# A batched matrix product in groups of four: order and run length of its loads, and which engine casts what

## The chip, the cores and the metric

The kernel runs on one core of a Trainium2 chip. Its engines each follow their own program: TensorE multiplies (PE in the profile, PEld for loading its stationary operand), VectorE (DVE), ScalarE (ACT) and GpSimd (POOL) do elementwise work, and SyncE (SP) here only issues transfers, which sixteen DMA engines carry out between the chip's main memory (HBM) and the core's memory (SBUF). Products arrive in PSUM. The engines meet at semaphores. The metric is device time in microseconds.

## What is computed

```python
# x: (8, 16, 256, 512) float32, weight: (8, 16, 512, 384) float32
def reference(x, weight):
    return np.matmul(x, weight).astype(np.float32)
```

That is 128 independent products of a 256x512 by a 512x384 matrix. The kernel reads 67.1 MB of x and 100.7 MB of weights, writes 50.3 MB, and multiplies in bf16.

## The kernel before

The 128 products are worked in NG = 32 groups of G = 4. Each SBUF tile has 128 partitions. A group's x is one transfer of 2 MB: partition p holds R = 8 consecutive rows of 512, so 32 partitions belong to each matrix (C = 32). A group's weights come in two transfers of 1.5 MB, two matrices each: partition p holds eight consecutive rows of 384, 12 KB, and 64 partitions belong to a matrix. A group's result is 1.5 MB, 12 KB per partition.

**Loads and stores (SyncE).** `on_sync` writes the order of the queue by hand. It first loads groups 0 to 3 (LAG = 4), then alternates load(n + 4) and store(n). `load` (L97 to L114) issues x (L101) and then the two halves of the weights (L109). There are two slots for x (XS = 2), four half slots for weights (WS = 4, so two groups) and four for results (OS = 4). Each issue waits until its slot is free: x until ScalarE has cast the x that lay there, weights until VectorE has cast theirs, a store (L122) until the group's result is copied. After the last load come stores 27 to 31; that of group 31 goes out in four pieces.

**VectorE** runs `prepare` for each group: eight casts of weights from fp32 to bf16 (L149, 64 partitions and 1536 elements each, the rows of a matrix being spread over all 128 partitions of w_bf), then four copies of transposed x from PSUM to x_t (L155), one for each pair of rows (T = 4). The casts wait for the weights' transfers, and for the multiplications of the group two before, which frees w_bf.

**TensorE** runs `multiply`: 16 transposes of x_bf (L168; pairs of bf16 numbers go through as one fp32 word), then 128 multiplications in four quarters (L182), with 32 columns of the array for each matrix. Quarter q waits for x_t's pair q and for the PSUM tile po (two of them), the first one also for all of the group's weight casts.

**ScalarE** copies each quarter from po to out_sb (`copy_out`, L196), and between quarters 1 and 2 casts the next group's x (`cast_x`, L131, two instructions of 2048 elements). There is one x_bf (BS = 1), so a cast of x waits for the transposes of the group before.

```python
        for n in range(rounds * U, NG):
            if n + LAG < NG:
                load(e, 0, NG, n + LAG)
            store(e, 0, NG, n, T if n == NG - 1 else 1)
```

Of the kernel before, what the change touches and what calls it, by code (L numbers as in the profile page):

```python
# [12 lines left out]
def kernel(  # L13
# [6 lines left out]
    nc = tc.nc  # L20
    P = 128

    b1, b2, M, K = x.shape
    _, _, _, N = weight.shape
    B = b1 * b2
    KO = K // P

    x_rows = x.rearrange("b1 b2 m k -> (b1 b2 m) k")
    w_rows = weight.rearrange("b1 b2 k n -> (b1 b2 k) n")
# [3 lines left out]
    bf16 = mybir.dt.bfloat16  # L33
# [6 lines left out]
    G = 4  # L40
    C = P // G
    R = G * M // P
    T = R // 2
    D = 2
    S = 2
    HP = P // D
    NG = B // G

    XS, WS, OS = 2, 2 * G // D, 4
    BS, TS, WBS = 1, 2, 2 * G  # L50
    PT, PO = 4, 2

    LAG = 4

    ctx.enter_context(tc.tile_critical(no_gpsimd_drain=True))  # L55

    def sbuf(name, shape, dtype, n):
        return [
            ctx.enter_context(nc.sbuf_tensor(f"{name}{s}", shape, dtype)) for s in range(n)
        ]  # L60
# [6 lines left out]
    def sems(name, n):  # L67
        return [tc.alloc_semaphore(f"{name}{s}") for s in range(n)]
# [2 lines left out]
    identity = sbuf("identity", [P, P], fp32, 1)[0]  # L71
    x_sb = sbuf("x_sb", [P, R, K], fp32, XS)

    x_bf = sbuf("x_bf", [P, R, S, HP, KO], bf16, BS)
    x_t = sbuf("x_t", [P, R, KO // 2, P, 2], bf16, TS)
    w_sb = sbuf("w_sb", [P, S * KO, N], fp32, WS)
    w_bf = sbuf("w_bf", [P, KO, N], bf16, WBS)
# [4 lines left out]

    id_done, x_cast, w_cast, t_made, t_copied, p_made, o_copied = (
        sems(name, 1)[0]
        for name in (
            "id_done", "x_cast", "w_cast", "t_made", "t_copied", "p_made", "o_copied"
        )
    )  # L90
    x_in, w_in, o_out = sems("x_in", XS), sems("w_in", WS), sems("o_out", OS)


    BIAS = 8


    def load(e, t, U, s):  # L97
        n = t * U + s
        if not isinstance(n, int) or n >= XS:
            e.wait_ge(x_cast, n + (1 - XS))  # L100
        e.dma_start(  # L101
            x_sb[s % XS][:],
            x_rows[bass.ds(n * (G * M), G * M)].rearrange("(p r) k -> p r k", r=R),
        ).then_inc(x_in[s % XS], 16)
        for d in range(G // D):
            slot = (s * (G // D) + d) % WS
            if not isinstance(n, int) or n >= 2:
                e.wait_ge(w_cast, n * (G * S) + ((d + 1) * D * S - 2 * G * S))  # L108
            e.dma_start(  # L109
                w_sb[slot][:],  # L110
                w_rows[bass.ds(n * (G * K) + d * (D * K), D * K)].rearrange(
                    "(p k) n -> p k n", k=S * KO
                ),
            ).then_inc(w_in[slot], 16)  # L114

    def store(e, t, U, s, pieces=1):
        n = t * U + s
        dram = o_rows[bass.ds(n * (G * M), G * M)].rearrange("(p r) n -> p r n", r=R)
        for q in range(pieces):
            rows = slice(q * R // pieces, (q + 1) * R // pieces)  # L120
            e.wait_ge(o_copied, n * T + ((q + 1) * T // pieces + BIAS))
            e.dma_start(out=dram[:, rows], in_=out_sb[s % OS][:, rows]).then_inc(  # L122
                o_out[s % OS], 16
            )

    def cast_x(e, t, U, s):
        n = t * U + s
        e.wait_ge(x_in[s % XS], (t * (U // XS) + s // XS) * 16 + 16)
        e.wait_ge(t_made, n * T + ((1 - BS) * T + BIAS))  # L129
        for h in range(S):  # L130
            ins = e.copy(  # L131
                out=x_bf[s % BS][:, :, h],
                in_=x_sb[s % XS][:].rearrange("p r (q s c) -> p r s q c", s=S, c=KO)[
                    :, :, h
                ],
            )
        ins.then_inc(x_cast, 1)

    def prepare(e, t, U, s):
        n = t * U + s  # L140
        e.wait_ge(p_made, n * T + (BIAS - T))
        for d in range(G // D):
            slot = (s * (G // D) + d) % WS
            e.wait_ge(  # L144
                w_in[slot], (t * (U * G // D // WS) + s * G // D // WS) * 16 + 16
            )
            for a in range(D):
                for h in range(S):
                    e.tensor_copy(  # L149
                        out=w_bf[(s * G + d * D + a) % WBS][h * HP : (h + 1) * HP],  # L150
                        in_=w_sb[slot][a * HP : (a + 1) * HP, h * KO : (h + 1) * KO, :],
                    ).then_inc(w_cast, 1)
        for q in range(T):
            e.wait_ge(t_made, n * T + (q + 1 + BIAS))
            e.tensor_copy(  # L155
                out=x_t[s % TS][:, 2 * q : 2 * q + 2],
                in_=pt[(s * T + q) % PT][:].bitcast(bf16),
            ).then_inc(t_copied, 1)

    def multiply(e, t, U, s):  # L160
        n = t * U + s
        words = x_bf[s % BS][:].rearrange("p r s q c -> p r (s q c)").bitcast(fp32)
        e.wait_ge(x_cast, n + 1)
        for q in range(T):
            e.wait_ge(t_copied, n * T + (q + 1 - PT + BIAS))
            for rr in range(2):
                for h in range(KO // 2):
                    ins = e.transpose(  # L168
                        pt[(s * T + q) % PT][:, rr, h, :],
                        words[:, 2 * q + rr, h :: KO // 2],  # L170
                        identity[:],
                    )
            ins.then_inc(t_made, 1)
        e.wait_ge(w_cast, n * (G * S) + G * S)
        for q in range(T):
            e.wait_ge(t_copied, n * T + (q + 1 + BIAS))
            e.wait_ge(o_copied, n * T + (q + 1 - PO + BIAS))
            for rr in range(2):
                for ko in range(KO):
                    for i in range(G):  # L180
                        mine = slice(i * C, (i + 1) * C)
                        ins = e.matmul(  # L182
                            po[(s * T + q) % PO][mine, rr, :N],
                            x_t[s % TS][:, 2 * q + rr, ko // 2, mine, ko % 2],
                            w_bf[(s * G + i) % WBS][:, ko, :],
                            start=(ko == 0),
                            stop=(ko == KO - 1),
                        )
            ins.then_inc(p_made, 1)

    def copy_out(e, t, U, s, q):
        n = t * U + s
        if q == 0:
            e.wait_ge(o_out[s % OS], (t * (U // OS) + s // OS) * 16 + 16)
        e.wait_ge(p_made, n * T + (q + 1 + BIAS))  # L195
        e.copy(  # L196
            out=out_sb[s % OS][:, 2 * q : 2 * q + 2, :],
            in_=po[(s * T + q) % PO][:, :, :N],
        ).then_inc(o_copied, 1)
# [7 lines left out]
    def on_sync(e):  # L207
        U = OS
        for n in range(LAG):
            load(e, 0, NG, n)  # L210
        rounds = (NG - LAG) // U
        with e.Fori(0, rounds) as t:
            for s in range(U):
                load(e, t, U, LAG + s)
                store(e, t, U, s)
        for n in range(rounds * U, NG):
            if n + LAG < NG:
                load(e, 0, NG, n + LAG)
            store(e, 0, NG, n, T if n == NG - 1 else 1)
        for s in range(OS):  # L220
            e.wait_ge(o_out[s], 16 + 16 * (NG // OS + (T - 1 if s == (NG - 1) % OS else 0)))

    def on_vector(e):
        U = 2
        e.sem_inc(t_copied, BIAS)
        with e.Fori(0, NG // U) as t:  # L226
            for s in range(U):
                prepare(e, t, U, s)

    def on_tensor(e):  # L230
        U = 2
# [8 lines left out]

    def on_scalar(e):
        U = OS
        e.sem_inc(o_copied, BIAS)
        for s in range(OS):
            e.sem_inc(o_out[s], 16)

        def step(t, U, s, more):
            for q in range(T):
                copy_out(e, t, U, s, q)
                if q == 1 and more:  # L250
                    cast_x(e, t, U, s + 1)

        cast_x(e, 0, NG, 0)
        with e.Fori(0, NG // U - 1) as t:
            for s in range(U):
                step(t, U, s, True)
        for n in range(NG - U, NG):
            step(0, NG, n, n < NG - 1)

    on_gpsimd(nc.gpsimd)  # L260
    on_sync(nc.sync)
    on_vector(nc.vector)
    on_tensor(nc.tensor)
    on_scalar(nc.scalar)


# [28 lines left out]
```

## Time and profile before

| | us |
|---|---|
| median of 14 runs (lowest, highest) | 519.77 (519.55, 520.37) |
| the profiled execution | 520.13 |
| its span, first to last instruction | 518.3 |
| mean transfer rate over the span | 421 GB/s |
| SP waits for x casts (ScalarE) / for weight casts (VectorE) | 258.9 / 135.5 |
| median time from issue to landing: weights / x / store | 27.6 / 25.9 / 30.6 |

Busy time says how long an engine had instructions in work; an engine waiting for data is idle. A line of groups gives the source line, engine and operation, what is written from what with shapes, the count, then busy time and the mean of one in ns, and after the second bar the idle time ahead of it and who ended it. The slices cut the span in 40 equal parts, with one digit of busy tenths for each.

### The profile page before, as it was taken

The numbers are of one execution on the slowest core, as the hardware profiler recorded it, in microseconds if no ns is written. First come the engines' busy times: TensorE is split into PE (matmuls) and PEld (weight loads), VectorE is DVE, ScalarE is ACT, GpSimd is POOL, SyncE is SP. The second block draws the span as 40 slices with busy tenths as digits, with TensorE's granted clock in tenths as the row PEclk, the third lists the DMA queues.
The fourth block names the chain that finished last, engine by engine and source line by source line (L and its number), as shares of the span: only waits on it lengthen the run. The fifth ranks groups of instructions, "written<-read, shape, count | busy, mean of one in ns | idle before, by whom it ended". The sixth has DMA issues, their size and how long they took to land.

```text
span 518.3 us, 11229 instructions
## 1 busy us (share of the span) xinstructions
PE 313.9 (61%) x4608; PEld 197.9 (38%) x4608; DVE 323.9 (62%) x384; ACT 212.9 (41%) x193; POOL 0.7 (0%) x6
## 2 busy tenths in 40 slices
PE   0587664576655666556756557665576655676653
PEld 0455443343433433333433334343344333443432
DVE  0788867655577555775556765557755577555670
ACT  3156462454324543245532445433455224553332
POOL 0000000000000000000000000000000000000000
PEclk9988896787867878688867878786888678776867
DMA  8999999999999999999999999999999999999995
GB/s 331 428 430 421 432 426 427 429 427 428 426 433 427 430 425 431 428 429 431 427 429 425 432 430 431 422 431 430 429 431 425 428 428 431 432 427 426 429 429 221
DMA packets 18869, 218.18 MB, mean 421 GB/s; under 512 B 2096, under 2 KB 2096, under 8 KB 2608
## 3 DMA queue, kind: packets, MB, share of 16 engines
q1 hardware_dynamic: 18864, 218.11, 99.2%
q8 instruction: 3, 0.05, 0.0%
q14 instruction: 2, 0.02, 0.0%
HBM read 167.77 MB, written 50.33 MB: 421 GB/s over the span
## 4 chain that ended last, share of the span: by engine, by line
DMA 77%; DVE 13%; PE 4%; issue 3%; SPq 1%; ACT 1%; DVEq 0%; ACTq 0%
DMA w_sb<-in_weight_dram 77%; DVE w_bf L149 12%; PE po L182 4%; ACT x_bf L131 0%; DVE x_t L155 0%; SPq L109 0%; SPq L101 0%; ACT out_sb L196 0%; DVEq L226 0%; DVEq L144 0%; SPq L108 0%; ACTq L129 0%; ACTq L195 0%; SPq L290 0%; SPq L55 0%
## 5 line engine op out<-in xcount | busy, mean ns | idle before, releaser
L149 DVE CAST w_bf<-w_sb 64x1536 bf16<-64x1536 f32 x256 | 244.4, 955 | 179.7 <-DMA w_sb<-in_weight_dram 167.0
L182 PE MATMUL po<-w_bf,x_t 128*32 128x384 bf16 x4096 | 232.0, 400 | 122.2 <-DVE x_t L155 122.2
L196 ACT COPY out_sb<-po 128x768 f32<-128x768 f32 x128 | 99.4, 803 | 289.5 <-PE po L182 289.5
L182 PEld LDWEIGHTS po<-w_bf,x_t 128*32 128x32 bf16 x4096 | 125.0, 116 | 225.9 <-DVE x_t L155 131.6
L168 PE MATMUL pt<-identity,x_bf 128*128 128x128 f32 x512 | 82.0, 323 | 74.0 <-ACT x_bf L131 74.0
L131 ACT CAST x_bf<-x_sb 128x2048 bf16<-128x2048 f32 x64 | 118.5, 1901 | 7.3 <-DMA x_sb<-in_x_dram 7.2
L168 PEld LDWEIGHTS pt<-identity,x_bf 128*128 128x128 f32 x512 | 72.9, 212 | 85.9 <-issue 85.9
L155 DVE COPY x_t<-pt 128x1024 bf16<-128x1024 bf16 x128 | 79.5, 683 | 1.0
L131 ACT ACT_TABLE_LOAD x1 | 1.3, 1283 | 1.3 <-PEq L232 1.3
masks.py:199 POOL TENSOR_SCALAR_AFFINE_SELECT identity<-identity 128x128 f32<-128x128 f32 x1 | 0.3, 292 | 0.2 <-POOL identity L202 0.2
L202 POOL MEMSET identity<- 128x128 f32 x1 | 0.2, 205 | 0.5 <-SPq L55 0.5
L279 POOL MEMSET const-bfloat16-1.0<- 128x1 bf16 x1 | 0.1, 102 | 0.0
L279 POOL MEMSET const-uint8-127<- 128x1 uint8 x1 | 0.1, 102 | 0.0
L279 POOL MEMSET const-float32-0.0<- 128x1 f32 x1 | 0.1, 99 | 0.2 <-issue 0.2
L279 POOL MEMSET const-float32-1.0<- 128x1 f32 x1 | 0.1, 99 | 0.0
## 6 DMA issues: line engine op xcount, KB each, us to landing
w_sb<-in_weight_dram SPq DMA_DIRECT2D x64, 1536.0 KB, 27.6
x_sb<-in_x_dram SPq DMA_DIRECT2D x32, 2048.0 KB, 25.9
out_dram<-out_sb SPq DMA_DIRECT2D x31, 1536.0 KB, 30.6
out_dram<-out_sb SPq DMA_DIRECT2D x4, 384.0 KB, 3.8
```

Source lines behind the costliest of these rows:

```text
L131: ins = e.copy(out=x_bf[s % BS][:, :, h], in_=x_sb[s % XS][:].rearrange("p r (q s c) -> p r s q c", s=S, c=KO)[:, :, h],)
L149: e.tensor_copy(out=w_bf[(s * G + d * D + a) % WBS][h * HP : (h + 1) * HP], in_=w_sb[slot][a * HP : (a + 1) * HP, h * KO : (h + 1) * KO, : ...
L155: e.tensor_copy(out=x_t[s % TS][:, 2 * q : 2 * q + 2], in_=pt[(s * T + q) % PT][:].bitcast(bf16),).then_inc(t_copied, 1)
L168: ins = e.transpose(pt[(s * T + q) % PT][:, rr, h, :], words[:, 2 * q + rr, h :: KO // 2], identity[:],)
L182: ins = e.matmul(po[(s * T + q) % PO][mine, rr, :N], x_t[s % TS][:, 2 * q + rr, ko // 2, mine, ko % 2], w_bf[(s * G + i) % WBS][:, ko, :], ...
L196: e.copy(out=out_sb[s % OS][:, 2 * q : 2 * q + 2, :], in_=po[(s * T + q) % PO][:, :, :N],).then_inc(o_copied, 1)
L202: e.memset(identity[:], 0.0).then_inc(id_done, 1)
L279: nc = _bacc.Bacc("TRN2", target_bir_lowering=False, num_devices=1)
```

## The change

One: a group's weights come in one transfer of 3 MB. Partition p holds sixteen consecutive rows, 24 KB, so 32 partitions belong to a matrix and its rows lie in S = 4 sets of KO = 4. The slots hold the same bytes (WS = 2). A group now takes sixteen weight casts of 32 partitions and 1536 elements. VectorE has the first CV = 12 of them and ScalarE the last CA = 4, with a semaphore each (`w_vcast`, `w_acast`). For the last group VectorE has 11 and ScalarE 5 (CL = 1).

Two: `cast_x` moves from ScalarE to VectorE, in four instructions of two rows (1024 elements), each with its own count of `x_cast`, ahead of the weight casts of its own group. Each waits for the same pair's transposes of the group before, and TensorE waits pair by pair.

Three: the copies from pt to x_t move from VectorE to ScalarE (`evacuate`). ScalarE's step for group n is: copy_out 0 and 1, a weight cast of group n + 1, copy_out 2, a cast, copy_out 3, two casts, the four copies to x_t of n + 1.

Four: the queue. The order is now x(n + 4), store(n), weights(n + 4). The last LATE = 2 groups are loaded without stores in between, so that stores 26 to 31 follow the last load.

```diff
-    D = 2
-    S = 2
-    HP = P // D
+    S = P // C
-    XS, WS, OS = 2, 2 * G // D, 4
+    XS, WS, OS = 2, 2, 4
-    LAG = 4
+    LAG, LATE = 4, 2
+    CA, CL = 4, 1
+    CV = G * S - CA
-    x_bf = sbuf("x_bf", [P, R, S, HP, KO], bf16, BS)
+    x_bf = sbuf("x_bf", [P, R, S, C, KO], bf16, BS)
...
+    def load_x(e, t, U, s):
         n = t * U + s
         if not isinstance(n, int) or n >= XS:
-            e.wait_ge(x_cast, n + (1 - XS))
+            e.wait_ge(x_cast, n * T + (1 - XS) * T)
...
+    def load_w(e, t, U, s):
+        n = t * U + s
+        if not isinstance(n, int) or n >= WS:
+            e.wait_ge(w_vcast, n * CV + (1 - WS) * CV)
+            e.wait_ge(w_acast, n * CA + (1 - WS) * CA)
+        e.dma_start(
+            w_sb[s % WS][:],
+            w_rows[bass.ds(n * (G * K), G * K)].rearrange("(p k) n -> p k n", k=S * KO),
+        ).then_inc(w_in[s % WS], 16)
...
+    def cast_x(e, t, U, s, q):
+        n = t * U + s
+        if q == 0:
+            e.wait_ge(x_in[s % XS], (t * (U // XS) + s // XS) * 16 + 16)
+        e.wait_ge(t_made, n * T + (q + 1 - T + BIAS))
+        rows = slice(2 * q, 2 * q + 2)
+        e.tensor_copy(
+            out=x_bf[s % BS][:, rows],
+            in_=x_sb[s % XS][:, rows].rearrange("p r (q s c) -> p r s q c", s=S, c=KO),
+        ).then_inc(x_cast, 1)
+
+    def cast_w(e, t, U, s, parts, first=True):
+        n = t * U + s
+        if first:
+            e.wait_ge(p_made, n * T + (BIAS - T))
+            e.wait_ge(w_in[s % WS], (t * (U // WS) + s // WS) * 16 + 16)
+        copy = e.tensor_copy if e is nc.vector else e.copy
+        for c in parts:
+            i, h = c // S, c % S
+            copy(
+                out=w_bf[(s * G + i) % WBS][h * C : (h + 1) * C],
+                in_=w_sb[s % WS][i * C : (i + 1) * C, h * KO : (h + 1) * KO, :],
+            ).then_inc(w_vcast if c < CV else w_acast, 1)
+
+    def evacuate(e, t, U, s):
         n = t * U + s
         e.wait_ge(p_made, n * T + (BIAS - T))
...
         for q in range(T):
             e.wait_ge(t_made, n * T + (q + 1 + BIAS))
-            e.tensor_copy(
+            e.copy(
                 out=x_t[s % TS][:, 2 * q : 2 * q + 2],
                 in_=pt[(s * T + q) % PT][:].bitcast(bf16),
             ).then_inc(t_copied, 1)
...
-        e.wait_ge(x_cast, n + 1)
         for q in range(T):
+            e.wait_ge(x_cast, n * T + (q + 1))
             e.wait_ge(t_copied, n * T + (q + 1 - PT + BIAS))
...
-        e.wait_ge(w_cast, n * (G * S) + G * S)
+        e.wait_ge(w_acast, n * CA + CA)
+        e.wait_ge(w_vcast, n * CV + CV)
...
         for n in range(LAG):
-            load(e, 0, NG, n)
-        rounds = (NG - LAG) // U
+            load_x(e, 0, NG, n)
+            load_w(e, 0, NG, n)
+        rounds = (NG - LATE - LAG) // U
         with e.Fori(0, rounds) as t:
             for s in range(U):
-                load(e, t, U, LAG + s)
+                load_x(e, t, U, LAG + s)
                 store(e, t, U, s)
+                load_w(e, t, U, LAG + s)
...
+        for n in range(NG - LATE, NG):
+            load_x(e, 0, NG, n)
+            load_w(e, 0, NG, n)
+        for n in range(NG - LATE - LAG, NG):
             store(e, 0, NG, n, T if n == NG - 1 else 1)
...
+        def step(t, U, s, parts):
+            for q in range(T):
+                cast_x(e, t, U, s, q)
+            cast_w(e, t, U, s, range(parts))
...
+        step(0, NG, NG - 2, CV)
+        step(0, NG, NG - 1, CV - CL)
...
+        def step(t, U, s, more=0):
+            parts = list(range(CV - more, CV + CA))
+            copy_out(e, t, U, s, 0)
+            copy_out(e, t, U, s, 1)
+            cast_w(e, t, U, s + 1, parts[:1])
+            copy_out(e, t, U, s, 2)
+            cast_w(e, t, U, s + 1, parts[1:2], False)
+            copy_out(e, t, U, s, 3)
+            cast_w(e, t, U, s + 1, parts[2:], False)
+            evacuate(e, t, U, s + 1)
```

More of the change, by code (lines that the diff above doesn't have):

```diff
@@ L80 @@
     po = psum("po", [P, 2, 512], fp32, PO)
-    id_done, x_cast, w_cast, t_made, t_copied, p_made, o_copied = (
+    id_done, x_cast, w_vcast, w_acast, t_made, t_copied, p_made, o_copied = (
         sems(name, 1)[0]
         for name in (
-            "id_done", "x_cast", "w_cast", "t_made", "t_copied", "p_made", "o_copied"
+            "id_done", "x_cast", "w_vcast", "w_acast",
+            "t_made", "t_copied", "p_made", "o_copied",
         )
@@ L94 @@
     BIAS = 8
-    def load(e, t, U, s):
+    def load_x(e, t, U, s):
         n = t * U + s
         if not isinstance(n, int) or n >= XS:
-            e.wait_ge(x_cast, n + (1 - XS))
+            e.wait_ge(x_cast, n * T + (1 - XS) * T)
         e.dma_start(
@@ L104, in load @@
         ).then_inc(x_in[s % XS], 16)
[L105 to L114, printed above, removed]
+    def load_w(e, t, U, s):
[7 more added lines that the diff above has]
+        ).then_inc(w_in[s % WS], 16)
     def store(e, t, U, s, pieces=1):
@@ L124, in store @@
             )
-    def cast_x(e, t, U, s):
+    def cast_x(e, t, U, s, q):
         n = t * U + s
[L128 to L139, printed above, removed]
+        if q == 0:
[19 more added lines that the diff above has]
+    def evacuate(e, t, U, s):
         n = t * U + s
         e.wait_ge(p_made, n * T + (BIAS - T))
[L142 to L152, printed above, removed]
         for q in range(T):
             e.wait_ge(t_made, n * T + (q + 1 + BIAS))
-            e.tensor_copy(
+            e.copy(
                 out=x_t[s % TS][:, 2 * q : 2 * q + 2],
@@ L209, in on_sync @@
         for n in range(LAG):
-            load(e, 0, NG, n)
-        rounds = (NG - LAG) // U
+            load_x(e, 0, NG, n)
+            load_w(e, 0, NG, n)
+        rounds = (NG - LATE - LAG) // U
         with e.Fori(0, rounds) as t:
             for s in range(U):
-                load(e, t, U, LAG + s)
+                load_x(e, t, U, LAG + s)
                 store(e, t, U, s)
-        for n in range(rounds * U, NG):
-            if n + LAG < NG:
-                load(e, 0, NG, n + LAG)
+                load_w(e, t, U, LAG + s)
+        for n in range(LAG + rounds * U, NG - LATE):
+            load_x(e, 0, NG, n)
+            store(e, 0, NG, n - LAG)
+            load_w(e, 0, NG, n)
+        for n in range(NG - LATE, NG):
+            load_x(e, 0, NG, n)
+            load_w(e, 0, NG, n)
+        for n in range(NG - LATE - LAG, NG):
             store(e, 0, NG, n, T if n == NG - 1 else 1)
@@ L224, in on_vector @@
         U = 2
-        e.sem_inc(t_copied, BIAS)
-        with e.Fori(0, NG // U) as t:
+        def step(t, U, s, parts):
+            for q in range(T):
+                cast_x(e, t, U, s, q)
+            cast_w(e, t, U, s, range(parts))
+        with e.Fori(0, NG // U - 1) as t:
             for s in range(U):
-                prepare(e, t, U, s)
+                step(t, U, s, CV)
+        step(0, NG, NG - 2, CV)
+        step(0, NG, NG - 1, CV - CL)
     def on_tensor(e):
@@ L242, in on_scalar @@
         U = OS
+        e.sem_inc(t_copied, BIAS)
         e.sem_inc(o_copied, BIAS)
@@ L245, in on_scalar @@
             e.sem_inc(o_out[s], 16)
[L247 to L254, printed above, removed]
-            for s in range(U):
-                step(t, U, s, True)
-        for n in range(NG - U, NG):
-            step(0, NG, n, n < NG - 1)
+        def step(t, U, s, more=0):
[8 more added lines that the diff above has]
+            evacuate(e, t, U, s + 1)
+        evacuate(e, 0, NG, 0)
+        cast_w(e, 0, NG, 0, range(CV, CV + CA))
+        rounds = (NG - 2) // U
+        with e.Fori(0, rounds) as t:
+            for s in range(U):
+                step(t, U, s)
+        for n in range(rounds * U, NG - 1):
+            step(0, NG, n, CL if n == NG - 2 else 0)
+        for q in range(T):
+            copy_out(e, 0, NG, NG - 1, q)
     on_gpsimd(nc.gpsimd)
```

## The prediction

> **What bounds the kernel now.** I read the engine table first, then the slices, the DMA queue and the chain.
>
> ```profile
> PE 313.9 (61%) x4608; PEld 197.9 (38%) x4608; DVE 323.9 (62%) x384; ACT 212.9 (41%) x193; POOL 0.7 (0%) x6
> ...
> DMA  8999999999999999999999999999999999999995
> GB/s 331 428 430 421 432 426 427 429 427 428 426 433 427 430 425 431 428 429 431 427 429 425 432 430 431 422 431 430 429 431 425 428 428 431 432 427 426 429 429 221
> ...
> q1 hardware_dynamic: 18864, 218.11, 99.2%
> ...
> DMA w_sb<-in_weight_dram 77%; DVE w_bf L149 12%; PE po L182 4%; ACT x_bf L131 0%; DVE x_t L155 0%; SPq L109 0%; SPq L101 0%; ACT out_sb L196 0%; DVEq L226 0%; DVEq L144 0%; SPq L108 0%; ACTq L129 0%; ACTq L195 0%; SPq L290 0%; SPq L55 0%
> ```
>
> No engine is over 62% busy, while the 16 DMA engines are at nine tenths or more in 38 of 40 slices. The chain runs through the weight loads. The groups and the waits agree: VectorE waits for weights in nearly every group, and SP, which has issued far ahead, waits only for buffers.
>
> ```profile
> L149 DVE CAST w_bf<-w_sb 64x1536 bf16<-64x1536 f32 x256 | 244.4, 955 | 179.7 <-DMA w_sb<-in_weight_dram 167.0
> L196 ACT COPY out_sb<-po 128x768 f32<-128x768 f32 x128 | 99.4, 803 | 289.5 <-PE po L182 289.5
> L131 ACT CAST x_bf<-x_sb 128x2048 bf16<-128x2048 f32 x64 | 118.5, 1901 | 7.3 <-DMA x_sb<-in_x_dram 7.2
> L155 DVE COPY x_t<-pt 128x1024 bf16<-128x1024 bf16 x128 | 79.5, 683 | 1.0
> ...
> x_sb<-in_x_dram SPq DMA_DIRECT2D x32, 2048.0 KB, 25.9
> ```
>
> A load lands 26 us after its issue, although 2 MB take 4.9 us at 429 GB/s: 21 us of other transfers stand before it. Last, the end, from the timeline and from windows of busy time (after the stretch and its length: PE, PEld, DVE, ACT, POOL, clock, DMA share, GB/s):
>
> ```profile
> 494.21 7.86 DVE L149 CAST w_bf<-w_sb 64x1536 bf16<-64x1536 f32 x8 [5.67 <-DMA w_sb<-in_weight_dram]
> ...
> 502.10 2.48 DVE L155 COPY x_t<-pt 128x1024 bf16<-128x1024 bf16 x4
> 502.84 7.28 PE L182 MATMUL po<-w_bf,x_t 128*32 128x384 bf16 x128 [4.23 <-DVE x_t L155]
> ...
> 510.18 0.80 ACT L196 COPY out_sb<-po 128x768 f32<-128x768 f32 x1 [0.50 <-PE po L182]
> ```
>
> ```profile
> 505.00:508.00 3.00, 3.00 (x56) 1.69 (x52) 0.00 (x0) 1.22 (x2) 0.00 (x0) 0.71 0.97 413
> ...
> 510.00:512.00 2.00, 0.12 (x4) 0.00 (x0) 0.00 (x0) 0.80 (x1) 0.00 (x0) 1.00 0.76 303
> 512.00:514.00 2.00, 0.00 (x0) 0.00 (x0) 0.00 (x0) 0.00 (x0) 0.00 (x0) 0.89 0.50 201
> 514.00:516.00 2.00, 0.00 (x0) 0.00 (x0) 0.00 (x0) 0.00 (x0) 0.00 (x0) 0.50 0.07 26
> ```
>
> The rate falls in steps because the 16 engines do not end together. The trace's landing events (16 for each transfer) show one engine behind the rest: by 1.1 us at the first x, by about 4 us at the last weights. On that engine store 30 lands at 513.19 and the four pieces of store 31 follow without a gap to 516.90 (3.71 us, as for any store). So one DMA engine is busy from the first load to the last store, and the span ends 1.4 us later. That is the bound; compute hides under it even at the end.
>
> [...]in its DMA records the median packet of 16 KB takes 611 ns, of 12 KB 460 ns, of 3 KB 121 ns. From 3 to 12 KB it is 339 ns, so 113 for 3 KB, and 8 ns are left for a packet (7 from the other pair); the 4-byte completion writes take 9 ns. [...]L149[...] goes every 0.985 us (7.89 for 8), but four L155 of 683 ns take 2.48, one per 0.60. [...]L131 has 1901 for 2048[...].
>
> **Part by part.**
>
> *24 KB runs.* A group's weights are 8 packets per DMA engine in place of 16, with one completion write less: 8 x 8 + 9 = 73 ns per group, 2.3 us over 32. Bytes stay. No trace shows a 24 KB packet; bounds 0 (the run is cut in two again) and 3.1 us (the slow engine loses some 0.1 us per group, 3.2 in all; if that hangs on its 32 packets per group, a quarter more, 0.8, goes). I take 2.3.
>
> *VectorE.* The price of halving a weight part's partitions: still 1536 elements per partition, so 955 ns each, but 16 parts for 8. Twelve stay here: 12 x 0.985 = 11.8 us per group[...]. The four x_t copies (2.5 us) leave and four x casts come, 1024 elements each[...], 2.5 us for four. No trace shows them here with runs of four elements; [...]lower bound 2.4, for L155's 683 has as many elements[...]. [...]I take 2.5. Sum 14.3 us per group against 10.4 before and 15.9 of DMA (6.82 MB at 429 GB/s). Covered, with 1.5 us to spare.
>
> *ScalarE.* Four copy_out at 0.80, four casts[...], four evacuations[...]: near 13 us per group, with waits inside. From matmul n-1's end to matmul n: copy_out 0.8, two casts 2.8, evacuation 1.0, so matmuls can follow at 7.3 + 4.7 = 12 us. Covered; without cover (over 15.9) every excess counts 32 times.
>
> *Queue and buffers.* On SP, w(n+2) waits for both engines' casts of n and goes out some 11.9 us after w(n) lands; behind it stand x(n+3) and a store. But when w(n) lands, x(n+1), a store, w(n+1), x(n+2) and a store are queued, 24 us: 12 are left. At the start, without stores, it is tighter. Weights 0 land at 17.2; VectorE ends them at 29.0, x(1) at 31.5, weights 1 at 43.3. Then w(3) goes out; x(3), in front of it, lands about 46.4 on the slow engine. A store piece lands 2.2 us after issue where nothing is queued, of which 1.0 is data, so 1.2 us of lead is wanted and 3.1 are there. Nothing lost. New waits on x_cast in multiply are met: x(n+1) is cast before matmul n.
>
> *The end.* This costs. LATE = 2 puts stores 26 and 27 behind the last loads, so x30, w30, x31, w31 come at 12.2 us per group, below VectorE's 14.3. Before, weights 29 landed at 465.82. Now store 25 is ahead of them (3.75) and 30 groups of runs are saved (2.2): 467.4. From there VectorE goes without a wait: 12 casts 11.8, x casts 2.5, 12 casts 11.8, x casts 2.5, 11 casts 10.8: 39.4, to 506.8. ScalarE with five parts of the last group: matmul 30 starts at 493.5 and ends 7.3 later at 500.8; copy_out 0.8, three casts 4.2, evacuation 1.0: 506.8, a tie. (copy_out 30 needs store 26 out, which lands near 495.5, as its product comes at 495.3.) Matmul 31 then starts at 506.8, where it was 502.84, and ends at 514.1 (7.28 as now); copy 0.8, issue 515.0, landing 2.2 to 2.5 later, 517.4. The slow DMA engine could have ended at 516.9 - 2.3 = 514.6, but waits for this. The end moves from 516.9 to 517.4, +0.5 us. What was saved in transfers is spent in the last two groups.
>
> The profiled execution took 520.13 (span 518.3, 1.8 around it), so it becomes 520.6; it lay 0.36 over the median of the runs, and against 519.77 I forecast 520.2.
>
> **Rivals.**
> - *A. Forecast*, the end's chain on VectorE and ScalarE: 519.0 to 521.7. For it: every term but the x cast rests on a row.
> - *B. The saving is kept*: the last store ends with the DMA floor, at 514.6, which is 2.3 us off the median: 517.5. It needs the end chain shorter by 2.8 us: the last matmul at full clock (the trace has such groups at 5.4, against 7.3: -1.9) and a dearer packet on the slow engine (-0.8). For it: matmul durations do vary from 5.4 to 8.2. Against: both ends of the list must come together. In part: 517.3 to 518.7.
> - *C. No saving in the packets*: w29 lands 2.2 us later and the same chain follows: 522.4; with x casts at 0.75 us another 0.5. For it: no 24 KB packet was seen. Range 521.7 to 524.
> - *D. VectorE becomes the bound*, through x_bf's casts. [...]It decides from (506.8 - 17.2 - 10.8)/31 = 15.4 us per group, an x cast of 0.95 us or a weight cast of 1.08.[...]
>
> **The numbers.** Chances: A 0.45, B 0.22, C 0.21, D 0.12. A change of 0.2% (1.04 us) is about what a measurement of this kernel can tell from none. A gives faster 0.04, same 0.28, slower 0.13; B faster 0.22; C slower 0.19, same 0.02; D slower. Together faster 0.26, same 0.30, slower 0.44. The range runs from B's floor, less 0.2 for the scatter of the runs, 517.3, to C's end, 524; D lies outside, with little else. The forecast's own range is A's.
>
> **What would show it.** w_sb packets: 32 issues of 3072 KB, 24 KB packets at about 912 ns. VectorE busy 32 x 14.2 = 455 us where it is 324, its wait for weights per group near 1.5 us and none in the last two. x cast row near 690 ns[...]. Weights 29 landing near 467.4 (469.6 says C). Last matmul from 506.8. A last store that follows its predecessor without a gap on every DMA engine says B. Wrong altogether: a GB/s row with slices under 420 in mid-run, which would mean that a buffer holds the queue.

## The result, and the profile after

The changed kernel took 526.23 us (median of 6 runs, 525.50 to 527.07) where the kernel before took 519.73 (28 runs). The ratio is 1.0125, with an interval from 1.0116 to 1.0135. It is 6.5 us slower; the forecast was 0.5 slower, with a range up to 524. The profiled execution took 526.89, with a span of 525.1; the forecast for it was 520.6.

From the page of the changed kernel, the engine table, the slices and the groups (after the bar busy us, mean ns of one; after the second bar idle us ahead and what ended it):

```profile
PE 306.0 (58%) x4608; PEld 205.0 (39%) x4608; DVE 443.6 (84%) x511; ACT 406.8 (77%) x386; POOL 0.7 (0%) x6
...
GB/s 337 429 426 383 394 426 429 434 431 436 431 424 424 433 431 432 429 427 432 435 432 432 427 426 434 431 437 431 431 422 432 435 431 428 427 435 402 381 396 125
...
L149 DVE CAST w_bf<-w_sb 32x1536 bf16<-32x1536 f32 x383 | 364.2, 951 | 54.9 <-DMA w_sb<-in_weight_dram 42.1
L149 ACT CAST w_bf<-w_sb 32x1536 bf16<-32x1536 f32 x129 | 189.4, 1468 | 2.6 <-DMA w_sb<-in_weight_dram 0.2
...
L159 ACT COPY x_t<-pt 128x1024 bf16<-128x1024 bf16 x128 | 120.3, 1025 | 0.8
...
L136 DVE CAST x_bf<-x_sb 128x1024 bf16<-128x1024 f32 x128 | 80.0, 688 | 11.1 <-DMA x_sb<-in_x_dram 10.1
```

The middle of the run is as forecast. The instructions take about what the forecast counted: 951 ns for a weight cast on VectorE (955), 688 for an x cast and 2.50 us for four (near 690 and 2.5), and on ScalarE 1468 for a cast and 1025 for a copy to x_t (1.4 and 1.0 us in the chain of the end). The forecast's figures for the x cast and for ScalarE's cast and copy were the author's estimates; no row of the profile before shows these instructions. VectorE, now 84% busy, still waits for weights: the group took 15.82 us, set by the transfers. The GB/s row holds the loss: two slices near the start (383, 394) and the last four (402, 381, 396, 125). Before, no slice between the first and the last was under 421.

The start, in windows of busy time of the changed kernel (columns as before: PE, PEld, DVE, ACT, POOL, clock, DMA share, GB/s):

```profile
40.00:45.00 5.00, 1.41 (x20) 0.88 (x24) 4.88 (x7) 4.95 (x5) 0.00 (x0) 0.86 0.99 406
45.00:50.00 5.00, 5.00 (x106) 3.16 (x100) 4.88 (x7) 3.82 (x5) 0.00 (x0) 0.80 0.88 329
50.00:55.00 5.00, 2.77 (x34) 2.21 (x24) 4.84 (x6) 4.90 (x6) 0.00 (x0) 1.00 0.97 410
55.00:60.00 5.00, 2.21 (x29) 1.26 (x33) 4.91 (x8) 4.98 (x5) 0.00 (x0) 0.73 0.98 343
```

Against the 429 GB/s of mid-run these four windows lack 5 x (23 + 100 + 19 + 86) = 1140 us x GB/s, which is 2.7 us of transfer. In the last of them the DMA engines are 98% busy and still move only 343 GB/s: the packets themselves take longer, those of 16 KB up to 1.58 us where the median is 0.61.

The timeline of the changed kernel (start, length, engine, line, count, then the idle time before and who ended it), first at the start, then at the end:

```profile
31.61 11.75 DVE L149 CAST w_bf<-w_sb 32x1536 bf16<-32x1536 f32 x12
...
43.38 0.33 SPq L115 DMA_DIRECT2D w_sb<-in_weight_dram  x1
...
470.41 11.76 DVE L149 CAST w_bf<-w_sb 32x1536 bf16<-32x1536 f32 x12 [1.57 <-DMA w_sb<-in_weight_dram]
...
496.90 7.06 PE L187 MATMUL po<-w_bf,x_t 128*32 128x384 bf16 x128 [4.58 <-ACT x_t L159]
...
498.81 10.76 DVE L149 CAST w_bf<-w_sb 32x1536 bf16<-32x1536 f32 x11
...
502.24 1.47 ACT L149 CAST w_bf<-w_sb 32x1536 bf16<-32x1536 f32 x1
503.73 0.80 ACT L201 COPY out_sb<-po 128x768 f32<-128x768 f32 x1
...
504.56 1.47 ACT L149 CAST w_bf<-w_sb 32x1536 bf16<-32x1536 f32 x1
505.93 0.78 ACT L201 COPY out_sb<-po 128x768 f32<-128x768 f32 x1
506.74 4.45 ACT L149 CAST w_bf<-w_sb 32x1536 bf16<-32x1536 f32 x3
511.21 3.76 ACT L159 COPY x_t<-pt 128x1024 bf16<-128x1024 bf16 x4
512.28 8.22 PE L187 MATMUL po<-w_bf,x_t 128*32 128x384 bf16 x128 [6.20 <-ACT x_t L159]
```

The weights of group 3 go out when group 1's casts are done, at 43.38, as forecast. But the matrix product of the last group starts at 512.28 where 506.8 was forecast. VectorE has ended its last casts at 498.81 + 10.76 = 509.57; the product waits for ScalarE's copies into x_t, and ScalarE has worked without a gap from 502.24 on: a cast, a copy, a cast, a copy, three casts, and the first of its copies to x_t, at whose end the product starts.

### The profile page after: what moved, and what is told of

Read it like the earlier page. It is cut to its first block, busy times and chain, and to the rows that moved or that the text cites. A ratio compares the mean times of both kernels' runs of the same rounds, so it can differ in the third digit from the quotient of the medians.

```text
span 525.1 us, 11607 instructions
## 1 busy us (share of the span) xinstructions
PE 306.0 (58%) x4608; PEld 205.0 (39%) x4608; DVE 443.6 (84%) x511; ACT 406.8 (77%) x386; POOL 0.7 (0%) x6
## 3 DMA queue, kind: packets, MB, share of 16 engines
q1 hardware_dynamic: 14256, 218.11, 98.0%
## 4 chain that ended last, share of the span: by engine, by line
DMA 48%; DVE 27%; issue 15%; ACT 5%; PE 4%; SPq 0%; DVEq 0%
DMA w_sb<-in_weight_dram 48%; DVE w_bf L149 25%; PE po L187 4%; ACT w_bf L149 3%; DVE x_bf L136 2%; ACT out_sb L201 1%; ACT x_t L159 1%; SPq L115 0%; SPq L105 0%; DVEq L145 0%; DVEq L243 0%; DVEq L134 0%; SPq L321 0%; SPq L58 0%
## 5 line engine op out<-in xcount | busy, mean ns | idle before, releaser
L149 DVE CAST w_bf<-w_sb 32x1536 bf16<-32x1536 f32 x383 | 364.2, 951 | 54.9 <-DMA w_sb<-in_weight_dram 42.1
L187 PE MATMUL po<-w_bf,x_t 128*32 128x384 bf16 x4096 | 236.7, 406 | 203.6 <-DVE w_bf L149 158.9
L187 PEld LDWEIGHTS po<-w_bf,x_t 128*32 128x32 bf16 x4096 | 139.9, 118 | 294.3 <-ACT x_t L159 193.9
L149 ACT CAST w_bf<-w_sb 32x1536 bf16<-32x1536 f32 x129 | 189.4, 1468 | 2.6 <-DMA w_sb<-in_weight_dram 0.2
L201 ACT COPY out_sb<-po 128x768 f32<-128x768 f32 x128 | 101.9, 796 | 99.1 <-PE po L187 97.7
L159 ACT COPY x_t<-pt 128x1024 bf16<-128x1024 bf16 x128 | 120.3, 1025 | 0.8
L136 DVE CAST x_bf<-x_sb 128x1024 bf16<-128x1024 f32 x128 | 80.0, 688 | 11.1 <-DMA x_sb<-in_x_dram 10.1
L172 PE MATMUL pt<-identity,x_bf 128*128 128x128 f32 x512 | 71.4, 294 | 11.0 <-DVE x_bf L136 11.0
L172 PEld LDWEIGHTS pt<-identity,x_bf 128*128 128x128 f32 x512 | 65.1, 209 | 20.8 <-issue 20.8
```

The costliest lines, as they stand in the source:

```text
L136: e.tensor_copy(out=x_bf[s % BS][:, rows], in_=x_sb[s % XS][:, rows].rearrange("p r (q s c) -> p r s q c", s=S, c=KO),).then_inc(x_cast, 1)
L149: copy(out=w_bf[(s * G + i) % WBS][h * C : (h + 1) * C], in_=w_sb[s % WS][i * C : (i + 1) * C, h * KO : (h + 1) * KO, :],).then_inc(w_vcas ...
L159: e.copy(out=x_t[s % TS][:, 2 * q : 2 * q + 2], in_=pt[(s * T + q) % PT][:].bitcast(bf16),).then_inc(t_copied, 1)
L172: ins = e.transpose(pt[(s * T + q) % PT][:, rr, h, :], words[:, 2 * q + rr, h :: KO // 2], identity[:],)
L187: ins = e.matmul(po[(s * T + q) % PO][mine, rr, :N], x_t[s % TS][:, 2 * q + rr, ko // 2, mine, ko % 2], w_bf[(s * G + i) % WBS][:, ko, :], ...
L201: e.copy(out=out_sb[s % OS][:, 2 * q : 2 * q + 2, :], in_=po[(s * T + q) % PO][:, :, :N],).then_inc(o_copied, 1)
```

## The experiments

Two losses could be read from this, so the first theory was: the queue runs dry at the start, and ScalarE is the last at the end. Against it stood that 24 KB packets are slow in themselves, that the order of the queue costs, and that the missing stores between the last loads cost or save. "Before" below is the median of the kernel before on the same chip as the run. The slow DMA engine is the one whose landing event of a transfer comes last of the sixteen; its lag is counted from the first of them. The events don't name the engine; that it is the same one all along is read from the steady growth of the lag.

**Something to transfer while group 3's weights wait.** Store 0 is put between x of group 3 and weights of group 3; the stores up to 24 so go one group earlier.

```diff
             load_x(e, 0, NG, n)
+            if n == LAG - 1:
+                store(e, 0, NG, 0)
             load_w(e, 0, NG, n)
...
-                store(e, t, U, s)
+                store(e, t, U, 1 + s)
...
-            store(e, 0, NG, n - LAG)
+            if n > LAG + rounds * U:
+                store(e, 0, NG, n - LAG)
```

> Store 0 goes out ahead of weights 3, and every store up to 24 one group earlier; the queue from group 29 on and all compute are unchanged. Theory 1 (the DMA queue runs dry once, before weights 3, and the late 2.9 us of weights 29 come from that): weights 3 find 3.7 us of store in front of them, no slice under 420 GB/s before the last fifth, no packet over 1.3 us between 40 and 60 us, weights 29 land near 467.7, and the time falls by 2.3 to 2.9 us, to about 523.6. Theory 2 (24 KB packets are slow by themselves): the slow packets stay, the time stays within 0.7 us of 526.2.

Measured: 525.56 us (524.79 to 526.98), before 519.81, ratio 1.0111 (1.0090 to 1.0132): 0.7 us better than the changed kernel, within the scatter of the two. In the windows of this run the rate from 40 to 60 us was 415 GB/s, where the four above average 372, and on the fast DMA engines weights 29 landed 1.9 us earlier. On the slow one, which decides, it was 1.05 us, since its lag was larger (5.7 us against 4.8). The end took the same course, by the timeline of this run:

```profile
511.61 8.05 PE L187 MATMUL po<-w_bf,x_t 128*32 128x384 bf16 x128 [6.22 <-ACT x_t L159]
```

It still waits for ScalarE, while VectorE had ended at 508.53. The direction is as expected, the size is a miss: the store was a partial cure. Packets of x of group 3, ahead of the store, took longer than usual in this run ("stretched" below), at 42 to 44 us: up to 1.35 us where 16 KB take 0.61.

**Take the fifth cast back from ScalarE** in the last group, so that VectorE has twelve and ScalarE four.

```diff
-    CA, CL = 4, 1
+    CA, CL = 4, 0
```

> CL = 0: VectorE casts 12 parts of the last group in place of 11, ScalarE 4 in place of 5. If ScalarE's row of work binds the start of the last multiplication (512.28, where VectorE had ended at 509.57): it starts some 1.4 us earlier, near 510.8, and the time falls by 1.0 to 1.5 us, to about 524.9. If VectorE binds it, as the forecast had it: 1.0 us slower, 527.2. If the DMA binds: no change.

Measured: 524.61 us (524.35 to 524.73), ratio 1.0090 (1.0073 to 1.0107), 1.6 us better than the changed kernel. From its timeline:

```profile
498.60 11.75 DVE L149 CAST w_bf<-w_sb 32x1536 bf16<-32x1536 f32 x12
...
507.22 2.96 ACT L149 CAST w_bf<-w_sb 32x1536 bf16<-32x1536 f32 x2
510.20 3.76 ACT L159 COPY x_t<-pt 128x1024 bf16<-128x1024 bf16 x4
511.26 7.06 PE L187 MATMUL po<-w_bf,x_t 128*32 128x384 bf16 x128 [4.58 <-ACT x_t L159]
```

VectorE has one cast more and now ends at 510.35, and yet the product starts a microsecond earlier, so VectorE was not what it waited for. From ScalarE's last copy of group 30 to the product it is 4.87 us (506.39 to 511.26) for 6.35, one cast less. The profiled execution gained another 1.2 us in the product's own length, 7.06 us for 8.22. That went with TensorE's granted clock, on average 0.76 over this product and 0.65 over the other, and isn't shown to come from the edit.

**The same bytes in 12 KB runs.** A group's weights go in two transfers of 12 KB per partition, at the same places in the queue.

```diff
-        e.dma_start(
-            w_sb[s % WS][:],
-            w_rows[bass.ds(n * (G * K), G * K)].rearrange("(p k) n -> p k n", k=S * KO),
-        ).then_inc(w_in[s % WS], 16)
+        rows = w_rows[bass.ds(n * (G * K), G * K)].rearrange("(p k) n -> p k n", k=S * KO)
+        for d in range(2):
+            half = slice(d * S * KO // 2, (d + 1) * S * KO // 2)
+            e.dma_start(w_sb[s % WS][:, half], rows[:, half]).then_inc(w_in[s % WS], 16)
```

> Each group's weights are two transfers of 12 KB per partition, into the same places; all else is the changed kernel. Theory 1 (longer packets save 8 ns each, 0.07 us per group): the period of a group on the DMA engines goes from 15.82 back to 15.88, and the time rises by 1.5 to 2.3 us, to about 528.2; the queue still runs dry before weights 3. Theory 2 (24 KB packets are slow by themselves, above all after a pause): the stretch from 44 to 60 us loses its slow packets and the time falls by 1 us or more.

Measured: 527.67 us (527.07 to 528.60), ratio 1.0150 (1.0133 to 1.0167), 1.4 us worse than the changed kernel. Its slices:

```profile
GB/s 332 429 419 390 422 428 431 429 424 432 429 428 429 430 433 425 427 428 428 427 434 427 428 428 428 434 425 429 429 428 431 430 426 429 429 429 398 395 375 123
```

The dip near the start and the slow end are there without any 24 KB packet, so the packets' length isn't needed for either. In mid-run the group takes 15.879 us for 15.817: the long runs save 0.062 us per group.

**Stores between the last loads.**

```diff
-    LAG, LATE = 4, 2
+    LAG, LATE = 4, 0
```

> LATE = 0: stores 26 and 27 stand ahead of weights 30 and 31 again. Last weights land near 502 instead of 496.2, and 11 casts of VectorE follow them, to 513.3. If early loads at the end bought much, 3 us or more slower. If, as I read the trace, the engines could not use them: 0 to 1.2 us slower, 526.2 to 527.4, with the second dry spot (482.5) gone.

Measured: 527.81 us (527.10 to 528.34), ratio 1.0157 (1.0140 to 1.0174), 1.6 us worse; the last weights landed at 501.05. With this end chain, LATE = 2 helps, somewhat more than expected.

**Both small cures**, the first two edits together.

> Store 0 ahead of weights 3 and CL = 0 together. They lie at the two ends of one chain, so the gains (0.7 and 1.6 us) should add up: 523.9. If the end is bound by something else once ScalarE is relieved, less: 524.6. Neither mends the second dry spot near 482 us.

Measured: 523.14 us (522.31 to 523.99), ratio 1.0071 (1.0056 to 1.0086). 3.1 us of the 6.5 are back, where the two alone gave 0.7 + 1.6. The remaining 3.4 need larger cures.

**Groups 0, 1, 30 and 31 as before.** These four load their weights in two 12 KB transfers and cast them in eight parts of 64 partitions on VectorE alone; x is still cast by VectorE and evacuated by ScalarE, and all other groups are those of the change.

```diff
+    ENDS = (0, 1, NG - 2, NG - 1)
+    E, H = 2, P // 2
...
+    def cast_w_halves(e, n):
...
+        for d in range(2):
+            seen = (n // WS) * 16 + 16 if d == 0 else (16 if n < WS else 32)
+            e.wait_ge((w_in, w_in2)[d][n % WS], seen)
+            for a in range(2):
+                for h in range(E):
+                    e.tensor_copy(
+                        out=w_bf[(n * G + d * 2 + a) % WBS][h * H : (h + 1) * H],
...
+        end(0)
+        end(1)
...
-                step(t, U, s, CV)
-        step(0, NG, NG - 2, CV)
-        step(0, NG, NG - 1, CV - CL)
+                step(t, U, 2 + s, CV)
+        end(NG - 2)
+        end(NG - 1)
```

> Groups 0, 1, 30 and 31 take their weights as the kernel before does (two transfers of 12 KB per partition, eight casts of 64 partitions, all on VectorE); groups 2 to 29 as the changed kernel. If the loss is VectorE's and ScalarE's sixteen weight casts per group where no cover is left, at the start and at the end: no dry spot, no slow packets after 10 us, weights 29 near 467.6, the last multiplication from about 500 to 503, the DMA engines busy to the last store, and of the packets' saving 2.0 us are kept: 517.8, with 519.3 if half of it goes astray. If 24 KB packets or VectorE's 84% in the middle are what costs: 522 or more.

Measured: 520.50 us (520.03 to 520.83, 21 runs), before 519.79, ratio 1.0014 (1.0007 to 1.0021). The dip at the start is gone: every slice from the second to the 37th is at 420 GB/s or more, and weights 29 landed at 468.33. But 2.7 us were missing to the expectation. Its timeline shows why:

```profile
490.72 2.78 PE L220 MATMUL po<-w_bf,x_t 128*32 128x384 bf16 x64 [0.58 <-ACT x_t L192]
...
498.03 1.50 ACT L234 COPY out_sb<-po 128x768 f32<-128x768 f32 x2 [5.48 <-DMA out_dram<-out_sb]
...
498.97 4.27 PE L220 MATMUL po<-w_bf,x_t 128*32 128x384 bf16 x64 [5.47 <-ACT out_sb L234]
```

The product of group 30 stops halfway, because ScalarE's copy of it has no slot: there are four result slots, and store 26 lay behind all loads (LATE = 2) and landed at 498.01. A faster end had met the next wait.

**The same, and LATE = 0.** In the last two groups the store goes between x and the weights again.

```diff
             load_x(e, 0, NG, n)
+            store(e, 0, NG, n - LAG)
             load_w_halves(e, n)
         e.sem_inc(w_acast, 2 * CA)
-        for n in range(NG - LATE - LAG, NG):
+        for n in range(NG - LAG, NG):
```

> As with the weights in halves for groups 0, 1, 30 and 31, but LATE = 0: stores 26 and 27 stand ahead of weights 30 and 31. In the run before, ScalarE's copy of group 30 waited 5.5 us for store 26, since there are four result slots. If that wait was all that was left: it goes, the last multiplication starts near 504.5 (second half of weights 31 at 500.3, four casts behind it), the DMA engines are busy to the last store near 516, and the time is 518.8. If the last weights' later landing costs as much as the wait did: 520.5.

Measured: 518.95 us (518.59 to 519.39, 21 runs), before 519.63, ratio 0.9987 (0.9980 to 0.9993). This version beats both kernels, the one before by 0.7 us. Its slices:

```profile
GB/s 332 427 437 422 429 430 422 435 431 441 426 422 431 436 432 436 425 425 433 431 435 424 428 434 431 438 430 429 423 431 435 430 430 426 433 432 424 430 429 196
```

And its timeline:

```profile
34.03 0.33 SPq L118 DMA_DIRECT2D w_sb<-in_weight_dram  x1
...
496.77 7.85 DVE L144 CAST w_bf<-w_sb 64x1536 bf16<-64x1536 f32 x8 [3.88 <-DMA w_sb<-in_weight_dram]
504.86 6.99 PE L220 MATMUL po<-w_bf,x_t 128*32 128x384 bf16 x128 [6.76 <-DVE w_bf L144]
```

Weights 3 go out at 34.03, 9.4 us earlier than in the changed kernel, and the rate doesn't fall until the end. There VectorE waits for transfers again, and the product waits for VectorE.

**Which end is worth what.** First the halves in groups 0 and 1 alone, with the end as in the changed kernel; then in 30 and 31 alone (with LATE = 0), with the start as in the changed kernel.

```diff
-    ENDS = (0, 1, NG - 2, NG - 1)
+    ENDS = (0, 1)
```

> The changed kernel with the weights in halves for groups 0 and 1 alone; its end as it was (LATE = 2, CL = 1). If the dry queue before weights 3 cost what the slow DMA engine lost there (2.0 to 2.7 us up to weights 29): 523.9, no slice under 415 GB/s before 470 us. If only what the first cure gave: 525.5.

```diff
-    ENDS = (0, 1, NG - 2, NG - 1)
+    ENDS = (NG - 2, NG - 1)
```

> The changed kernel with the weights in halves for groups 30 and 31 alone and LATE = 0; its start as it was, so the queue runs dry before weights 3. Start and end lie on one chain, so what the other kernel of this call leaves of the 7.3 us between 526.2 and 518.95 should be found here: 521.0 to 521.5. If the end is bound by the DMA engines' lateness from the start alone: 524 or more.

Measured: 524.76 us (523.45 to 525.70), before 519.66, ratio 1.0091 (1.0071 to 1.0112), for the start; 520.91 us (520.14 to 522.41, 13 runs), ratio 1.0023 (1.0014 to 1.0031), for the end. Start 1.5 and end 5.3 make 6.8 of the 7.3 us between the changed kernel and the best version, so the two nearly add up. With the start cured, the wait for weights 29 ended at 468.30 for 470.41. With the end cured, the slices keep the dip and lose the slow end, as the page and the timeline of that run show:

```profile
GB/s 341 433 435 404 383 429 425 435 432 433 429 424 434 432 433 433 426 429 432 435 433 428 426 432 432 440 427 429 424 437 427 434 432 425 433 435 424 426 432 193
```

```profile
506.50 7.56 PE L220 MATMUL po<-w_bf,x_t 128*32 128x384 bf16 x128 [6.41 <-DVE w_bf L144]
```

**The order alone.** The kernel before, with nothing but the order x, store, weights.

```diff
             x_rows[bass.ds(n * (G * M), G * M)].rearrange("(p r) k -> p r k", r=R),
         ).then_inc(x_in[s % XS], 16)
+        if between:
+            between()
...
-                load(e, t, U, LAG + s)
-                store(e, t, U, s)
+                load(e, t, U, LAG + s, lambda: store(e, t, U, s))
```

> The kernel before with the order x, store, weights alone, everything else as it was. The last weights then land one store (3.8 us) later and the end's chain with them: weights 31 at 501.5, first half at 497.9, last multiplication 506.6 in place of 502.84. The slow DMA engine still has four stores behind the last weights, to 516.9, and the last piece is issued at 514.8, so 0.3 to 0.6 us slower: 520.2. If the order helps the transfers themselves (a store followed by weights): faster, 519.3 or less.

Measured: 523.04 us (522.88 to 523.84), before 519.79, ratio 1.0069 (1.0053 to 1.0084). It costs 3.3 us where 0.4 was expected. Its timeline:

```profile
500.56 7.86 DVE L151 CAST w_bf<-w_sb 64x1536 bf16<-64x1536 f32 x8 [5.78 <-DMA w_sb<-in_weight_dram]
...
509.20 7.28 PE L184 MATMUL po<-w_bf,x_t 128*32 128x384 bf16 x128 [4.32 <-DVE x_t L157]
```

The last weights' first half landed at 500.47 for 494.11, 6.4 us later. One store more ahead of them is 3.7. The rest is the slow DMA engine: by the landing events its lag grew 0.195 us per group between x of groups 6 and 27, for 0.103 before; over 28 groups that is 2.6.

**The best version with the order of before**, so that a store follows the weights.

```diff
                 load_x(e, t, U, LAG + s)
-                store(e, t, U, s)
                 load_w(e, t, U, LAG + s)
+                store(e, t, U, s)
```

> The same with the queue in the order of the kernel before: x, weights, store. The last weights then land one store (3.8 us) earlier than in the other kernel of this call and the last multiplication starts near 500.7, while the DMA engines have the same to do: if they bind, the same 518.8 within 0.4. If the end's chain still binds, faster than the other by 1 us or more. If the order x, store, weights is worth something in the middle: slower than the other.

Measured: 527.24 us (526.34 to 527.68), before 519.63, ratio 1.0147 (1.0131 to 1.0162), 8.3 us worse than with x, store, weights. From its timeline:

```profile
497.26 2.50 DVE L167 CAST x_bf<-x_sb 128x1024 bf16<-128x1024 f32 x4 [3.90 <-DMA x_sb<-in_x_dram]
...
509.09 6.87 PE L220 MATMUL po<-w_bf,x_t 128*32 128x384 bf16 x128 [7.71 <-DVE w_bf L144]
```

VectorE waits for x of group 31 until 497.26. The fast DMA engines keep their 15.81 us per group; on the slow one the lag grows 0.369 us per group, to 10.2 us at x of group 27. In all runs of the change with the store ahead of the weights it grew by 0.04 to 0.09. The order x, store, weights, which costs 3.3 us in the kernel before, is worth 8.3 in the best version.

**That run with 12 KB weights.** Is it the 24 KB packets ahead of a store? The groups between the ends get two transfers of 12 KB per partition, as above.

```diff
-        e.dma_start(
-            w_sb[s % WS][:],
-            w_rows[bass.ds(n * (G * K), G * K)].rearrange("(p k) n -> p k n", k=S * KO),
-        ).then_inc(w_in[s % WS], 16)
+        for d in range(2):
+            half = slice(d * S * KO // 2, (d + 1) * S * KO // 2)
+            e.dma_start(w_sb[s % WS][:, half], rows[:, half]).then_inc(
+                (w_in, w_in2)[d][s % WS], 16
+            )
```

> This is e10 (x, weights, store; halves in the first and last two groups) with every other group's weights in two transfers of 12 KB per partition as in e3, at the same places. Theory R (the slow DMA engine falls behind because a store follows packets of 24 KB): its lag returns to some 0.1 us per group as in the kernel before, which has 12 KB packets and this order; the time is that of e9 plus 28 x 0.062 for the packets, 518.95 + 1.7 = 520.7, up to 521.5. Theory O (what decides is not the length of the runs but where stores and weights stand, or when they are issued): the lag stays near 0.37 per group, and the time is that of e10 or up to 1.7 more, 527 to 529. In between: both have a part.

Measured: 529.45 us (528.89 to 529.92), before 519.56, ratio 1.0191 (1.0174 to 1.0208), which is theory O, just beyond the upper end of its range. The lag grows 0.405 us per group, and VectorE waits for x of group 31 until 499.28.

So the length of the runs is not what decides between the orders. The kernel before has this order and this length, with a lag of 0.103; what differs in mid-run is which engine casts what, and when.

The DMA records show where the lag grows. Around 210 us, one DMA engine's store packets, six in one run and seven in the other, take 493 to 540 ns for 460. This comes back in every group: between 100 and 420 us the excess of all 12 KB packets of over 485 ns adds up to 0.38 us per group in each of these two runs, to 0.15 in the run with the order alone, and to 0.03 in the kernel before and in the best version.

Casts of weights beside the stores do not explain it. In the run with the order alone no weight cast runs beside any of the stretched packets. In the best version the slow engine's stores (the 21 that could be followed in the records) ran beside VectorE's weight casts from end to end, and took only 0.06 us more than eight times 460 ns. What sets the three runs apart is TensorE: 95 to 100% of their stretched time lies beside its multiplications, which fill 46 or 47% of the time from 100 to 420 us, while the stores followed in the best version and in the kernel before have none beside them. No run moved the multiplications alone, so they are not shown to be the cause.

## Why the prediction was wrong

**Where it failed: the start.** The step reads "x(3), in front of it, lands about 46.4 on the slow engine" and "1.2 us of lead is wanted and 3.1 are there. Nothing lost." Issue and landing were right (43.38, 46.65). But the lead was taken on the slow engine alone, and on fourteen of the sixteen x of group 3 had landed between 44.8 and 45.6. The first packets of weights 3 started 1.1 to 3 us after the issue, and many of them took 1.2 to 1.7 us where 24 KB take 0.91 in mid-run; between 55 and 59 us x of group 4 had such packets too. Two things thus failed: lead had to be counted for each engine, and the lead that is wanted was read from the landing of one small store. Weights 29 landed at 470.32, forecast 467.4: 2.9 us, near the 2.7 of the windows. In e11_halves_at_start, where weights 3 go out earlier, the dip is gone and weights 29 landed at 468.20, so 2.1 of the 2.9 belong to the start; the other 0.8 stays open. That edit changes the first casts and transfers along with the time of issue. e1_store0_before_w3, which changes the queue alone, filled most of the dip, so the dry queue is well supported as its cause, though no single edit isolates it.

**Where it failed: the end on ScalarE.** The step reads "copy_out 0.8, three casts 4.2, evacuation 1.0: 506.8, a tie." From the end of matmul 30 to the start of matmul 31 that is 6.0 us; it took 8.3 (503.96 to 512.28). The working had let ScalarE stand ready for the last copy when the product ends. In fact it copies quarter 1 at 501.42, casts, copies quarter 2 at 503.73 and casts again, and comes to the last copy only at 505.93. With matmul 30's start 0.5 later than forecast after the landing and its length 0.2 shorter, this is 2.6 us more. VectorE's own chain was right: 39.2 us, forecast 39.4. But it wasn't what the product waited for, which e2_last_cast_back shows from the other side.

**Mis-sized: the last product.** 8.22 us where 7.28 was carried over from before, 0.9. The runs in which it went through without a stop gave 6.9 to 8.2. The clock that TensorE was granted explains the spread: its mean over the product was 0.65 in the changed kernel, 0.73 before, and 0.76 in e2_last_cast_back with its 7.06 us, and length times clock is 5.3 to 5.4 us in all three. The forecast carried a length over without its clock.

Together, 2.9 + 2.6 + 0.9, less 0.1 at the last copy and landing, make 6.3, which is 526.89 against the 520.6 forecast for the profiled execution.

**What held.** The 24 KB packet takes 912 ns, and a group on the fast engines 0.065 us less than before (forecast 0.073); e3_two_12KB_runs gives 0.062. Two packets of 12 KB take 920 ns (medians of 460), so one of 24 KB saves 8, as the forecast had estimated from the medians before, and rival C falls. Its sign came all the same, weights 29 at 470.32 where "469.6 says C": two causes had the same sign, and the packets decide between them. The sign of being wrong altogether, slices under 420, came too, not in mid-run but near the start (383 and 394) and at the end. Rival D falls with the x cast of 688 ns, where it would have decided from 0.95 us: VectorE waits for weights in 24 groups, 42 us in all. ScalarE is covered in mid-run. B, the saving kept whole, needed a short end; only with both ends cured and LATE = 0 does some of it appear, 0.7 of 2.3 us.

**What was not priced.** The order x, store, weights had no price of its own beside the store that it moves. It costs 3.3 us by itself (e8_order_alone), where 2.6 of the 6.4 us by which the last weights landed later are the slow DMA engine's. Once VectorE and ScalarE share the casts it saves 8.3 (e10_halves_order_before), through the same engine. The forecast had taken that engine's lag as it was.

**What stays open.** Three things. Why packets are stretched after a pause (1.2 to 1.7 us for 0.91), and again 10 us later with the engines 98% busy. Why one DMA engine falls behind in one order and not in the other. The length of the runs is excluded (e13_order_before_12KB), weight casts beside the store are neither needed nor enough, and TensorE's multiplications beside it fit all the runs compared but were not tried alone. And why its lag took half of what e1_store0_before_w3 had gained.

## What to carry to other kernels

A change that pays in the steady state has to be priced again in the first and the last groups: here coarser loads and casts left the queue dry once and put the longest serial row on the last group, and giving four of 32 groups their finer form, with the stores back between the last loads, turned 6.5 us of loss into 0.7 of gain. Count the lead of a transfer on the engine that runs out first, and walk an engine's program instruction by instruction between two events before calling it a tie. Carry a product's length over only together with its clock (in the kernel before, 5.38 us at a mean granted clock of 1.00 and 8.24 at 0.64). Try an order of transfers together with the schedule of the engines that runs beside it, since it can have the opposite sign alone (here 3.3 us worse, against 8.3 better in the best version).

## What had not been expected of the hardware

After the DMA engines of the changed kernel had run dry at 45 us, many of the next 24 KB packets took 1.2 to 1.7 us for 0.91, and a second burst followed at 55 to 59 us (16 KB packets up to 1.58 us for 0.61), while the engines were 98% busy. By their shares in the four windows from 40 to 60 us the engines idled 0.9 us, and the windows lack 2.7 us of transfer: more was lost than the idle time. One of the sixteen DMA engines falls behind by 0.04 to 0.41 us per group, at equal bytes (218.11 MB in the queue of every run), depending on the order of the queue and on the schedule beside it, and between e9_halves_no_late and e10_halves_order_before that went with 8.3 us. Where it fell behind fastest, 95% or more of the stretch lay beside TensorE's multiplications; in e9_halves_no_late its stores ran beside weight casts without them, and took 0.06 us more than usual each.
